# Attention's input product in pairs of column chunks: four of five 1024-column units by a seven-product scheme

## The chip, the cores and the metric

One core of a Trainium2 chip runs one program, a two-layer encoder of 256 tokens and width 2048. TensorE (PE) multiplies into PSUM, VectorE (DVE) and ScalarE (ACT) do the elementwise work, GpSimd (POOL) some of it, and DMA queues bring every weight from HBM. The metric is the device time of the whole program in microseconds, the median of three runs.

## The reference, cut to what matters

The change touches the first product of layer 0: the normalised input times `w_in` of 5264 columns, which are queries Q (2048), keys K (512), values V (512), the indexer's queries (2048), its key (128) and 16 indexer weights.

```python
hn = rmsnorm(h, norm_mix_g[i])
...
proj = hn @ w_in                       # 256 x 2048 times 2048 x 5264, float32
q = proj[..., :o0].reshape(B, S, N_HEADS, HEAD_DIM)
k = proj[..., o0:o1].reshape(B, S, N_KV, HEAD_DIM)
v = proj[..., o1:o2].reshape(B, S, N_KV, HEAD_DIM)
qi = proj[..., o2:o3].reshape(B, S, IDX_HEADS, IDX_DIM)
ki = proj[..., o3:o4]
wi = proj[..., o4:].astype(jnp.float32) * (IDX_HEADS ** -0.5 * IDX_DIM ** -0.5)
q = rope(q, positions, HEAD_DIM); k = rope(k, positions, HEAD_DIM)
ki = layernorm(ki, kidx_g, kidx_b)
qi = rope(qi, positions, IDX_ROPE); ki = rope(ki, positions, IDX_ROPE)
# indexer scores -> the 64 best keys of each token -> softmax attention over those -> @ w_out
```

After it come a squared-ReLU MLP, a gated embedding, then layer 1 with a convolution in place of attention, and the final norm.

## The kernel before, in words

Activations stand in SBUF transposed, as blocks of 128 features by 256 tokens (two token halves t = 0, 1). A float32 product is made of three fp32r matmuls: activation and weight are each split in a high part (`xh`, `wh`) and a low part (`xl`, `wl`), and high x high, high x low and low x high are added in PSUM. The high part of a weight tile is made by ACT (L322), the low part by DVE (L323), both in `halves`. A weight tile `raw` is 128 x 2 x 512 floats (512 KB); there are nine raw buffers (`RAWS`) and six pairs of split buffers (`SPLITS`).

`gemm` (L369) makes one chunk of up to 512 columns: 16 feature blocks x 2 token halves x 3 = 96 matmuls and 8 weight tiles. `pair_gemm` (L215), which before serves the MLP and the gate products only, makes two chunks at once. Of the 16 feature blocks 8 go through a seven-product scheme (Strassen's form by Winograd): pairs of blocks, token halves and chunks form 2 x 2 block matrices, and seven products on sums of activations and sums of weights replace eight. That is 7 x 4 x 3 = 84 matmuls for 96; the other 8 blocks take 96 as always, so a pair takes 180 for 192. The weights' sums are made in the raw tiles, by a DMA that adds while it writes (issued by POOL, L261) or by DVE (L263); each sum is split again, so a pair has 22 splits for 16. The activations' sums (L191 to L203, class `Sums`) are made once per activation.

In attention, before, all ten chunks go through `gemm`: V, K, a chunk of 400 columns (256 indexer queries, the indexer's key, the 16 weights), the indexer's queries in 512 + 512 + 512 + 256, then Q in four of 512. The input `x` comes in four chunks of 512 features; each is transposed on PE (L428), scaled and split by ACT (L382) and DVE (L383), while the first product already runs. The constant vectors of later layers are loaded by `vectors` (L146 to L157): five small DMAs on ACT's queue (L150), then one transpose on PE (L155) and a copy on DVE (L156).

Every engine works its own queue in order. The order of the work is set by `defer` and `step` (a piece of work runs so many steps later) and then by the framework's scheduler, which lays out each engine's list when the program is built. What stands on an engine behind a waiting instruction waits too; ACT's DMA issues are in ACT's list.

## Time and profile before

| | |
|---|---|
| median of three runs | 2248.43 us (2247.61 to 2248.62) |
| the profiled execution | 2248.04 us |
| its span, first to last instruction | 2246.3 us |
| PE busy | 2224.4 us, 99% of the span |
| DVE busy | 1874.4 us, 83% |
| ACT busy | 1432.1 us, 64% |
| mean granted TensorE clock | 0.998 |

A profile row gives an engine, a line of the kernel, the operation, what it writes `<-` reads, and shapes. The matmuls overlap, so the duration of one is no price; the distance from start to start is. The same holds in a small way on ACT and DVE, where the next instruction starts some 0.1 us before the last one's recorded end. Idle time stands in brackets with what ended it.

### The profile page before, as it was taken

What the parts mean: (1) busy time and instruction counts of PE and PEld (TensorE: products, weight loads), DVE (VectorE), ACT (ScalarE), POOL (GpSimd) and SP (SyncE); (2) the same over time, 40 slices, a digit from 0 to 9 for tenths busy, and PEclk for the clock granted to TensorE, in tenths of its full rate; (3) what the DMA queues carried; (4) which work ended last, traced back from release to release, by engine and by line L of the source; (5) the groups of instructions that cost most, each with busy time, mean ns of one, the idle gap of its engine ahead of it and who ended that gap; (6) DMA issues with size and microseconds to landing.
All of it is one profiled execution on the core that took longest, in us unless ns stands there. A gap on an engine that the chain in (4) does not pass through costs nothing.

```text
span 2246.3 us, 29595 instructions
## 1 busy us (share of the span) xinstructions
PE 2224.4 (99%) x10366; PEld 1847.5 (82%) x10366; DVE 1874.4 (83%) x2516; ACT 1432.1 (64%) x1920; POOL 428.6 (19%) x313
## 2 busy tenths in 40 slices
PE   9999999999999999999999999999999999999998
PEld 7888778888888888888898887888888888888886
DVE  5658657988888888889868999789889889889987
ACT  6545546765765765766765744577567577577675
POOL 0201210111011011011139872111111101101012
PEclk9999999999999999999999999999999999999999
DMA  8655446887887887887767552677877877877884
GB/s 278 198 150 171 148 128 169 224 249 204 234 242 203 238 240 202 243 232 202 205 194 226 181 175 67 201 199 201 275 205 202 271 201 209 270 196 216 237 245 121
DMA packets 268021, 463.42 MB, mean 206 GB/s; under 512 B 16340, under 2 KB 62308, under 8 KB 267744
## 3 DMA queue, kind: packets, MB, share of 16 engines
q1 hardware_dynamic: 225840, 381.88, 50.9%
q0 software_dynamic: 39168, 75.51, 20.1%
q10 hardware_dynamic: 2864, 4.15, 0.6%
q8 instruction: 81, 1.33, 0.2%
q14 instruction: 68, 0.56, 0.1%
HBM read 459.38 MB, written 2.10 MB: 205 GB/s over the span
## 4 chain that ended last, share of the span: by engine, by line
PE 93%; DVE 4%; issue 1%; DMA 1%; ACT 1%; POOL 0%; SPq 0%; POOLq 0%; DVEq 0%; ACTq 0%
PE pm L238 42%; PE at L238 21%; PE pm L347 8%; PE pm L349 8%; PE pm L348 8%; PE pt L763 1%; DVE at L950 1%; PE at L808 1%; DVE wl L323 1%; PE pt L428 1%; PE at L612 0%; PE at L659 0%; PE at L689 0%; DMA work<-in_b_w_dw 0%; DMA raw<-in_a_w_in 0%
## 5 line engine op out<-in xcount | busy, mean ns | idle before, releaser
L322 ACT ACTIVATE wh<-raw 128x1024 fp32r<-128x1024 f32 (+2 forms) x1032 | 1058.8, 1040 | 621.8 <-PE at L238 187.8
L323 DVE TENSOR_TENSOR wl<-raw,wh 128x1024 fp32r<-128x1024 f32 (+1 forms) x955 | 1146.5, 1223 | 267.1 <-ACT wh L322 250.6
L261 POOL DMA_DIRECT2D raw<-in_mlp_w x128 | 155.1, 1212 | 1203.1 <-DVE wl L323 1076.3
L238 PE MATMUL pm<-wl,xhA 128*128 128x512 f32 x504 | 197.7, 392 | 0.0
L238 PE MATMUL pm<-wl,xhB 128*128 128x512 f32 x504 | 197.5, 392 | 0.0
L238 PE MATMUL pm<-wh,xlB 128*128 128x512 f32 x504 | 196.4, 391 | 0.0
L238 PE MATMUL pm<-wh,xlA 128*128 128x512 f32 x504 | 196.4, 391 | 0.0
L238 PE MATMUL pm<-wh,xhB 128*128 128x512 f32 x504 | 192.5, 392 | 0.0
L238 PE MATMUL pm<-wh,xhA 128*128 128x512 f32 x504 | 192.3, 393 | 0.0
L347 PE MATMUL pm<-wh,xhA 128*128 128x512 f32 (+2 forms) x480 | 184.1, 388 | 1.4 <-ACT xhA L382 0.6
L349 PE MATMUL pm<-wh,xlA 128*128 128x512 f32 (+2 forms) x480 | 183.6, 387 | 0.5 <-DVE xlA L1041 0.5
L348 PE MATMUL pm<-wl,xhA 128*128 128x512 f32 (+2 forms) x480 | 183.8, 384 | 0.0
L263 DVE TENSOR_TENSOR raw<-raw 128x1024 f32<-128x1024 f32 x144 | 175.5, 1220 | 1.0
L323 POOL TENSOR_TENSOR wl<-raw,wh 128x1024 fp32r<-128x1024 f32 (+1 forms) x77 | 158.3, 2079 | 30.2 <-ACT wh L322 29.1
L347 PE MATMUL pm<-wh,xhB 128*128 128x512 f32 (+1 forms) x448 | 163.1, 365 | 0.0
L348 PE MATMUL pm<-wl,xhB 128*128 128x512 f32 (+1 forms) x448 | 162.0, 362 | 0.0
L349 PE MATMUL pm<-wh,xlB 128*128 128x512 f32 (+1 forms) x448 | 161.8, 363 | 0.0
L950 DVE SCALAR_TENSOR_TENSOR at<-u,wdw,at 128x256 f32<-128x256 f32 x402 | 160.5, 483 | 0.0
L238 PE MATMUL at<-wh,xlA 128*128 128x512 f32 x360 | 140.9, 391 | 0.0
L238 PE MATMUL at<-wh,xhA 128*128 128x512 f32 x360 | 140.8, 391 | 0.0
L238 PE MATMUL at<-wh,xlB 128*128 128x512 f32 x360 | 140.8, 391 | 0.0
L238 PE MATMUL at<-wh,xhB 128*128 128x512 f32 x360 | 140.7, 391 | 0.0
(228 smaller groups left out, 3951.1 us busy)
## 6 DMA issues: line engine op xcount, KB each, us to landing
raw<-in_mlp_w SPq DMA_DIRECT2D x448, 512.0 KB, 5.4
raw<-in_mlp_w POOLq DMA_DIRECT2D x128, 512.0 KB, 6.4
raw<-in_a_w_in SPq DMA_DIRECT2D x72, 512.0 KB, 4.1
raw<-in_ple_w_gate SPq DMA_DIRECT2D x56, 512.0 KB, 5.6
raw<-in_b_w_pw SPq DMA_DIRECT2D x96, 256.0 KB, 3.1
raw<-in_a_w_out SPq DMA_DIRECT2D x32, 512.0 KB, 3.7
raw<-in_b_w_pw SPq DMA_DIRECT2D x32, 512.0 KB, 4.3
raw<-in_ple_w_gate POOLq DMA_DIRECT2D x16, 512.0 KB, 6.2
```

The costliest lines, as they stand in the source:

```text
L238: nc.tensor.matmul(bank[v], l, r, start=v not in begun, stop=bool(left[v] == 0 or (last and j == 2)), skip_group_check=v in again)
L261: nc.gpsimd.dma_start(r, piece(*rows(other, q)), accum_op=ALU.add)
L263: nc.vector.tensor_tensor(r, r, raw(other, q), op=ALU.add)
L322: recent[0] = nc.scalar.activation(wh, r, AF.Copy).ins
L323: (low or nc.vector).tensor_tensor(wl, r, wh.bitcast(F32), op=ALU.subtract)
L347: nc.tensor.matmul(pm[t][:, :n], a, wh[:, i], start=k + i == 0, stop=False)
L348: nc.tensor.matmul(pm[t][:, :n], a, wl[:, i], start=False, stop=False)
L349: nc.tensor.matmul(pm[t][:, :n], b, wh[:, i], start=False, stop=k + i == kt - 1)
L428: nc.tensor.transpose(pt[:, k, t, :], h[:, t, (kk + k) * P:(kk + k + 1) * P], ident)
L763: nc.tensor.transpose(pt[:, k, t, :], both[t][:, 2 * j + k, :], ident)
L808: nc.tensor.matmul(pp, l, r[:, k], start=k == 0 and j == 0, stop=k == 1 and j == 2)
L950: nc.vector.scalar_tensor_tensor(dst, src, w, z, op0=ALU.mult, op1=ALU.add)
```

## The change: what it does

The ten chunks become five units. K and V, the first and the second half of the indexer's queries, and the first half of Q each are a pair of chunks through `pair_gemm`; the second half of Q stays two `gemm` chunks, and the chunk of 400 columns shrinks to 144 (the indexer's key and the weights), since the 256 columns of indexer queries go into a pair. A new class `Beside` holds the activation's blocks as before, and five of the seven sums beside them, in the tiles that attention's output takes later. The paired feature blocks are the last eight instead of the first eight. The first pair begins with two plain groups (`begin=2`), and `x` is loaded in the order 0, 2, 3, 1. `rotated` and `two_chunks` take a finished bank through a copy on ACT and a sum on DVE to the old rotation; `LATE` puts the second head group's attention four steps later. One of the two `at` banks is held by a pair, and part of the indexer's dot products (`dots`) go to the transpose banks. The squares for the norm are put off by some steps.

In the whole program PE has 10182 matmuls for 10230: in attention 48 more of 512 columns, 96 of 144 in place of 96 of 400, and 96 of 256 gone. DVE and ACT have 32 more splits of a full weight tile each (and 8 of 144 columns for 8 of 400 and 8 of 256), DVE 16 more sums of weight tiles, 16 more sums of banks and some 28 more small instructions; POOL issues 16 more adding DMAs.

Two places of the order matter below. The first is ACT's list around the five vector loads (L150 before, L153 now). Before, they stand between the scaled copies and splits of the first weight tiles (`xhA` is the high part of a transposed `x` block, `wh` of a weight tile, `work ... ssq` a square for the norm):

```order
L322 ACTIVATE wh_273<-raw_271 128x1024
L401 ACTIVATE work_307,ssq_111<-h_79 128x512
L401 ACTIVATE work_309,ssq_111<-h_79 128x512
L150 DMA work_77<-in_norm_mlp_g 32x128
L382 ACTIVATE xhA_109<-pt_226,vcol_87 128x256
L382 ACTIVATE xhA_109<-pt_235,vcol_87 128x256
L150 DMA work_77<-in_b_ln_g 16x128
L322 ACTIVATE wh_313<-raw_311 128x1024
L150 DMA work_77<-in_b_ln_b 16x128
L150 DMA work_77<-in_b_b_dw 16x128
L150 DMA work_77<-in_b_b_pw1 32x128
L322 ACTIVATE wh_331<-raw_329 128x1024
```

Now ACT's list has them behind its twelfth split, behind eight squares and behind two copies of banks (L615), the last of which reads the bank `pm_152` that PE fills with the third of the seven products of the first pair:

```order
L450 ACTIVATE work_368,ssq_111<-h_79 128x512
L450 ACTIVATE work_388,ssq_111<-h_79 128x512
L615 ACTIVATE held_332<-at_149 128x512
L450 ACTIVATE work_390,ssq_111<-h_79 128x512
L615 ACTIVATE held_428<-pm_152 128x512
L153 DMA work_77<-in_norm_mlp_g 32x128
L153 DMA work_77<-in_b_ln_g 16x128
L153 DMA work_77<-in_b_ln_b 16x128
L153 DMA work_77<-in_b_b_dw 16x128
L153 DMA work_77<-in_b_b_pw1 32x128
L371 ACTIVATE wh_480<-raw_296 128x1024
```

So the five loads have moved from the first five weight tiles of the program to the middle of the first pair, behind an instruction that waits for PE.

The second is PE's list around the transpose that those loads feed (L155 before, L158 now). Before:

```order
L348 MATMUL pm_382<-wl_441,xhA_109 128x512
L349 MATMUL pm_382<-wh_440,xlA_110 128x512
L347 MATMUL pm_383<-wh_440,xhA_109 128x512
L348 MATMUL pm_383<-wl_441,xhA_109 128x512
L349 MATMUL pm_383<-wh_440,xlA_110 128x512
L155 MATMUL at_456<-ident_80,work_77 128x112
L347 MATMUL pm_382<-wh_461,xhA_109 128x512
L348 MATMUL pm_382<-wl_462,xhA_109 128x512
L349 MATMUL pm_382<-wh_461,xlA_110 128x512
L347 MATMUL pm_383<-wh_461,xhA_109 128x512
```

`pm_382` and `pm_383` are banks of the second chunk, whose matmuls go on behind the transpose. Now:

```order
L281 MATMUL at_149<-wh_298,xlB_114 128x512
L281 MATMUL pm_152<-wl_413,xhB_113 128x512
L281 MATMUL pm_152<-wh_412,xlB_114 128x512
L281 MATMUL pm_152<-wh_412,xhB_113 128x512
L281 MATMUL pm_152<-wl_413,xhB_113 128x512
L281 MATMUL pm_152<-wh_412,xlB_114 128x512
L158 MATMUL at_492<-ident_80,work_77 128x112
L281 MATMUL at_149<-wh_452,xhB_113 128x512
L281 MATMUL at_149<-wl_453,xhB_113 128x512
L281 MATMUL at_149<-wh_452,xlB_114 128x512
L281 MATMUL at_149<-wh_452,xhB_113 128x512
L281 MATMUL at_149<-wl_453,xhB_113 128x512
```

`at_492` is the transpose's bank; `pm_152` is the bank of the copy above and `at_149` the pair's fourth bank, which goes on with a twice summed weight tile (`raw_283` in the split `wh_452`). The transpose has moved from behind 132 matmuls of 512 columns to directly behind the last matmul into `pm_152`: before it now stand 18 warming transposes, 33 transposes of inputs and 72 matmuls of 512 columns, and between the last matmul that the copy waits for and the transpose stands nothing.

The diff, cut to its core:

```diff
@@ -79,8 +81,9 @@
         return ps_tr.tile([P, NB], F32, name="pt", tag="tr")
 
     def at_tile(which=None):
+
         if which is None:
-            turns[0] ^= 1
+            turns[0] = 1 - (turns[0] if unit_bank[0] is None else unit_bank[0])
             which = turns[0]
         return ps_at.tile([P, NB], F32, name="at", tag=f"at{which}")
 
...
+    def five(kk, pt, g):
+
+        y, z, v = work(4, P), work(4, P), work(2, P)
+        for k, dst in ((0, v), (1, z[:, 1:3, :])):
...
+        tt(y[:, 1, :], x11, y[:, 3, :], op=ALU.subtract)
+        tt(z[:, 0, :], x12, y[:, 1, :], op=ALU.subtract)
+        return y, z
+
+    class Beside:
+
+
+
+        def __init__(self, x, other):
+            self.x = x
+            self.five = []
+            for p in "hl":
+                v = acts.tile([P, KT, S], F32R, name="x" + p + other, tag="x" + p + other).rearrange("p k s -> p (k s)")
+                self.five.append(v[:, :5 * SP * P].rearrange("p (m i f) -> p m i f", m=5, i=SP))
+            self.paired, self.plain = KT - 2 * SP, range(KT - 2 * SP)
+
+        def block(self, part, k, t):
+            return self.x[part][:, k, t * P:(t + 1) * P]
+
+        def sums(self, part, m, i):
+            return self.five[part][:, m, i, :] if m < 5 else self.block(part, self.paired + 2 * i + 1, m - 5)
+
+        def put(self, kk, pt, g):
+            put_blocks([v[:, kk:kk + 2, :] for v in self.x], pt, g[:, kk:kk + 2])
+            if kk >= self.paired:
+                y, z = five(kk, pt, g)
+                i = (kk - self.paired) // 2
+                for m, n, src in ((0, 4, y), (4, 1, z[:, :1, :])):
+                    split(self.five[0][:, m:m + n, i, :], self.five[1][:, m:m + n, i, :], src)
...
-    def pair_gemm(x, src, taken, extras=(), apart=False):
+    def pair_gemm(x, src, take, extras=(), apart=False, begin=0):
...
-        bank = {"x": at_tile(), "y": mm_tile(), "v": mm_tile(), "z": mm_tile()}
+        mine = 1 - (turns[0] if unit_bank[0] is None else unit_bank[0])
+        unit_bank[0] = mine
+
+        def taken(what, b):
+            take(what, b)
+            if what == "x" and unit_bank[0] == mine:
+                unit_bank[0] = None
+
+        bank = {"x": at_tile(mine), "y": mm_tile(), "v": mm_tile(), "z": mm_tile()}
         begun, again, left = set(), set(), {"x": 3 * SP, "y": SP, "v": SP, "z": 2 * SP}
         for v in left:
-            left[v] += KT - 2 * SP
+            left[v] += len(x.plain)
             left[v] *= 3
...
         def rows(name, q):
-            return range(2 * q.start + (name in "cd"), 2 * q.stop, 2), int(name in "bd")
+            return range(x.paired + 2 * q.start + (name in "cd"), x.paired + 2 * q.stop, 2), int(name in "bd")
...
-        ks = groups(2 * SP, KT - 2 * SP)
+        ks = groups(x.plain.start, len(x.plain))
+        n1 = [lambda r=r: plain(0, r) for r in ks]
+
+        def more(n):
+            for _ in range(n):
+                n1.pop(0)()
+
+        more(begin)
         seven(0, "x", "a", part="x1")
         add("a", "b")
         seven(5, "y", "c")
-        for r in ks[:-2]:
-            plain(0, r)
+        more(len(n1) - 2 if not begin else 1)
         seven(3, "z", "a", part="z1")
         add("a", "d")
         seven(4, "z", "d")
         add("d", "b")
         seven(1, "x", "a", part="x2")
         add("a", "c")
-        plain(0, ks[-2])
+        more(len(n1) - 1)
         seven(6, "v", "a")
         seven(2, "x", "d", part="x3")
-        plain(0, ks[-1])
+        more(len(n1))
         for r in ks:
             plain(1, r)
         return rest
...
@@ -461,19 +510,22 @@
...
+    xS = Beside(xA, "B")
+
     def first(c):
-        h_half(4 * c, xA, gcol["mix0"])
-        h_half(4 * c + 2, xA, gcol["mix0"])
-        defer(SQ_LAG, lambda: norm.add(c, recent[0]))
+        h_half(4 * c, xS, gcol["mix0"])
+        h_half(4 * c + 2, xS, gcol["mix0"])
 
     load_x(0)
     pv = at_tile()
     nc.tensor.transpose(pv[:, :32], vrow[0][:32, :], ident[:32, :32])
     nc.vector.tensor_copy(vcol[:, :32], pv[:, :32])
     first(0)
-    for c in range(1, 4):
-        defer(2 * c - 1, lambda c=c: load_x(c))
-        defer(2 * c, lambda c=c: first(c))
+    for c, load, turn in ((2, 1, 2), (3, 2, 2), (1, 3, 4)):
+        defer(load, lambda c=c: load_x(c))
+        defer(turn, lambda c=c: first(c))
+    for c in range(4):
+        defer(4 + c, lambda c=c: norm.add(c, recent[0]))
     defer(8, vectors)
...
+        def two_chunks(n0, ends, begin=0):
+
+            rs = {}
+
+            def taken(what, bank):
+                if what in EARLY:
+                    rs[EARLY[what]] = held(4, P)
+                    nc.scalar.activation(rs[EARLY[what]].rearrange("p h d -> p (h d)"), bank, AF.Copy)
+                    return
+                (t, n), r = WHERE[what], rs[what]
+                rf = r.rearrange("p h d -> p (h d)")
+                nc.vector.tensor_tensor(rf, bank, rf, op=ALU.subtract if what in MINUS else ALU.add)
+                ends[n](t, r)
+            pair_gemm(xS, blocks(w_in, n0, 2 * NB), taken, begin=begin)
...
+        def rotated(rot, make, then):
+
+            toks = {}
+
+            def end(t, r):
+                nc.scalar.activation(r, r, AF.Copy, scale=norm0[t])
+                rope(r, t, 4, rot)
+                toks[t] = r
+                if len(toks) == TT:
+                    dst = make()
+                    turn_heads(toks, dst)
+                    then(dst)
+            return end
...
         norm0 = norm
         vv = att.tile([P, TT, NB], F32, name="vv")
-        pm = gemm(xA, blocks(w_in, V0))
-
-        def values(pm=pm):
-            for t in range(TT):
...
         kT = att.tile([P, 4, S], F32, name="kT")
-        pm = gemm(xA, blocks(w_in, K0))
-        defer(0, lambda pm=pm: heads(pm, 128, kT))
+        defer(12, angles)
+
+        def values(t, r):
+            nc.scalar.activation(vv[:, t, :], r.rearrange("p h d -> p (h d)"), AF.Copy, scale=norm0[t])
+        two_chunks(K0, (rotated(128, lambda: kT, lambda dst: None), values), begin=2)
...
-        pm = gemm(xA, blocks(w_in, KI0 - 256, 400))
+        pm = gemm(xA, blocks(w_in, KI0, 144))
...
         defer(0, index_keys)
-        defer(0, lambda pm=pm: heads(pm, 64, qT_last[:, 2:4]))
...
         def dots(j, qT, t):
             per = NB // KS[t]
             for q in range(0, 4, per):
-                pa = at_tile()
+                pa = at_tile() if q == 0 else tr_tile()
...
-        for j in range(4):
-            pm = gemm(xA, blocks(w_in, QI0 + j * NB, NB if j < 3 else 256))
-
-            def index_heads(j=j, pm=pm):
-                qT = att.tile([P, 4, S], F32, name="qT", bufs=2) if j < 3 else qT_last
-                heads(pm, 64, qT if j < 3 else qT[:, :2])
-                defer(3, lambda: dots(j, qT, 0))
-                defer(4, lambda: dots(j, qT, 1))
-            defer(0, index_heads)
...
+        def index_heads(j):
+            def then(qT):
+                defer(3, lambda: dots(j, qT, 0))
+                defer(4, lambda: dots(j, qT, 1))
+                if j == 3:
+                    defer(5, lambda: select(0))
+                    defer(6, lambda: select(1))
+            return rotated(64, head_tile, then)
+
+        def head_tile():
+            return att.tile([P, 4, S], F32, name="qT", bufs=2)
+
+        for j in range(0, 4, 2):
+            two_chunks(QI0 + j * NB, (index_heads(j), index_heads(j + 1)))
...
+        def attention(g, qT, late=0):
             def go(t):
                 lgs = logits(g, qT, t)
                 defer(2, lambda: attend(g, lgs, t))
-            defer(2, lambda: go(0))
-            defer(3, lambda: go(1))
+            defer(2 + late, lambda: go(0))
+            defer(3 + late, lambda: go(1))
+
+        def query_heads(g, pm):
+            qT = head_tile()
+            heads(pm, 128, qT)
+            attention(g, qT)
...
-        for g in range(N_KV):
+        two_chunks(Q0, [rotated(128, head_tile, lambda qT, g=g: attention(g, qT, LATE * g)) for g in range(2)])
+        xB = xpair("B")
+        for g in range(2, N_KV):
             pm = gemm(xA, blocks(w_in, Q0 + g * NB))
             defer(0, lambda g=g, pm=pm: query_heads(g, pm))
```

## Rows read from the trace of the kernel before

**Rows 1.** the page: share of the chain that ended last, by engine

```profile
PE 93%; DVE 4%; issue 1%; DMA 1%; ACT 1%; POOL 0%; SPq 0%; POOLq 0%; DVEq 0%; ACTq 0%
```

**Rows 2.** windows: stretch, length, busy us (count) per engine, clock, DMA share, GB/s

```profile
8.00:25.00 17.00, 14.99 (x58) 11.42 (x58) 10.66 (x16) 12.02 (x26) 0.00 (x0) 1.00 1.00 362
40.00:330.00 290.00, 290.00 (x1416) 242.42 (x1415) 187.81 (x303) 150.88 (x244) 50.69 (x58) 1.00 0.54 165
500.00:540.00 40.00, 40.00 (x178) 33.11 (x177) 34.62 (x34) 22.47 (x23) 4.85 (x5) 1.00 0.86 252
```

**Rows 3.** timeline of PE, 512, 400, 256 columns, transposes, float32: start, length

```profile
111.68 0.39 PE L347 MATMUL pm<-wh,xhA 128*128 128x512 f32 x1
...
114.18 0.39 PE L349 MATMUL pm<-wh,xlA 128*128 128x512 f32 x1
...
62.10 0.34 PE L348 MATMUL pm<-wl,xhA 128*128 128x400 f32 x1
...
66.07 0.34 PE L349 MATMUL pm<-wh,xlA 128*128 128x400 f32 x1
...
153.54 0.28 PE L348 MATMUL pm<-wl,xhA 128*128 128x256 f32 x1
...
156.18 0.28 PE L349 MATMUL pm<-wh,xlA 128*128 128x256 f32 x1
...
20.60 1.04 PE L428 MATMUL pt<-ident,h 128*128 128x128 f32 x8
...
120.51 1.02 PE L612 MATMUL at<-kiT,qT 128*128 128x256 f32 x4
```

**Rows 4.** timeline of ACT in the first 35 us: rows that give distances

```profile
1.76 0.45 ACTq L490 DMA_DIRECT2D kg<-in_a_kidx_g  x1
...
7.66 0.46 ACT L382 ACTIVATE xhA<-pt,vcol 128x256 fp32r<-128x256 f32 x1
...
12.17 0.82 ACT L382 ACTIVATE xhA<-pt,vcol 128x256 fp32r<-128x256 f32 x2
...
31.53 2.94 ACT L322 ACTIVATE wh<-raw 128x1024 fp32r<-128x1024 f32 x3
```

**Rows 5.** groups of ACT over the span: count, busy, mean ns

```profile
L744 ACT ACTIVATE held<-at 128x512 f32<-128x512 f32 x48 | 28.4, 592 | 19.8 <-PE at L238 19.8
...
L401 ACT ACTIVATE work<-h 128x512 f32<-128x512 f32 x40 | 24.9, 622 | 10.8 <-DVE h L826 7.0 <-DMA h<-in_x 3.7
```

**Rows 6.** DMA issues: queue, count, KB, us to landing

```profile
pos_i<-in_positions ACTq DMA_DIRECT2D x1, 1.0 KB, 2.3
work<-in_norm_mix_g SPq DMA_DIRECT2D x1, 16.0 KB, 1.7
work<-in_norm_mlp_g ACTq DMA_DIRECT2D x1, 16.0 KB, 6.2
```

**Rows 7.** timeline of PE: its 73rd matmul of 512 columns, and a gap

```profile
33.58 0.73 PE L347 MATMUL pm<-wh,xhA 128*128 128x512 f32 x2
34.88 0.50 PE L347 MATMUL pm<-wh,xhA 128*128 128x512 f32 x1 [0.57 <-ACT xhA L382]
```

**Rows 8.** windows around the fall of the granted clock, columns as in rows 2

```profile
1370.00:1372.70 2.70, 1.48 (x8) 0.67 (x6) 2.09 (x8) 0.00 (x0) 0.00 (x0) 1.00 0.00 0
1372.70:1376.20 3.50, 2.93 (x13) 2.66 (x14) 2.18 (x5) 1.10 (x3) 0.69 (x1) 0.51 0.00 0
```

**Rows 9.** timeline of DVE in the first 40 us

```profile
8.15 0.48 DVE L383 SCALAR_TENSOR_TENSOR xlA<-pt,vcol,xhA 128x256 fp32r<-128x256 f32 x1 [2.21 <-ACT xhA L382]
8.96 0.88 DVE L383 SCALAR_TENSOR_TENSOR xlA<-pt,vcol,xhA 128x256 fp32r<-128x256 f32 x2 [0.32 <-ACT xhA L382]
...
37.41 2.36 DVE L323 TENSOR_TENSOR wl<-raw,wh 128x1024 fp32r<-128x1024 f32 x2
```

**Rows 10.** groups of DVE over the span: sums of activations, and their low parts

```profile
L197 DVE TENSOR_TENSOR work<-work 128x128 f32<-128x128 f32 x48 | 13.7, 286 | 0.0
...
L380 DVE TENSOR_TENSOR xlB<-work,xhB 128x512 fp32r<-128x512 f32 x24 | 16.0, 684 | 0.0
```

More of the change, by code (lines that the diff above doesn't have):

```diff
@@ L54 @@
 HELD = 8
+LATE = 4
 WHERE = {"y": (0, 0), "z": (0, 1), "v": (1, 0), "x": (1, 1)}
@@ L73, in encoder @@
     turns = [0]
+    unit_bank = [None]
     def mm_tile():
@@ L177, in __init__ @@
             self.rest = [v[:, n:].rearrange("p (k s) -> p k s", s=S) for v in self.main]
+            self.paired, self.plain = 0, range(2 * SP, KT)
         def block(self, part, k, t):
@@ L190, in put @@
                 return
-            y, z, v = work(4, P), work(4, P), work(2, P)
-            for k, dst in ((0, v), (1, z[:, 1:3, :])):
-                nc.scalar.activation(dst, pt[:, k], AF.Copy, scale=g[:, kk + k:kk + k + 1] if g is not None else 1.0)
-            x11, x21, x12, x22 = v[:, 0, :], v[:, 1, :], z[:, 1, :], z[:, 2, :]
-            tt = nc.vector.tensor_tensor
-            nc.vector.tensor_scalar(y[:, 0, :], x11, -1.0, None, op0=ALU.mult)
-            tt(y[:, 2, :], x21, x11, op=ALU.subtract)
-            tt(y[:, 3, :], x21, x22, op=ALU.subtract)
-            tt(y[:, 1, :], x11, y[:, 3, :], op=ALU.subtract)
-            tt(z[:, 0, :], x12, y[:, 1, :], op=ALU.subtract)
+            y, z = five(kk, pt, g)
             i = kk // 2
@@ L203, in put @@
                 split(dst[0][:, :, i, :], dst[1][:, :, i, :], src)
+    def five(kk, pt, g):
+        y, z, v = work(4, P), work(4, P), work(2, P)
+        for k, dst in ((0, v), (1, z[:, 1:3, :])):
+            nc.scalar.activation(dst, pt[:, k], AF.Copy, scale=g[:, kk + k:kk + k + 1] if g is not None else 1.0)
+        x11, x21, x12, x22 = v[:, 0, :], v[:, 1, :], z[:, 1, :], z[:, 2, :]
+        tt = nc.vector.tensor_tensor
+        nc.vector.tensor_scalar(y[:, 0, :], x11, -1.0, None, op0=ALU.mult)
+        tt(y[:, 2, :], x21, x11, op=ALU.subtract)
+        tt(y[:, 3, :], x21, x22, op=ALU.subtract)
+        tt(y[:, 1, :], x11, y[:, 3, :], op=ALU.subtract)
[16 more added lines that the diff above has]
+            if kk >= self.paired:
+                y, z = five(kk, pt, g)
+                i = (kk - self.paired) // 2
+                for m, n, src in ((0, 4, y), (4, 1, z[:, :1, :])):
+                    split(self.five[0][:, m:m + n, i, :], self.five[1][:, m:m + n, i, :], src)
     def put_blocks(x, pt, g):
@@ L418, in put @@
     def put(x, kk, pt, g=None):
-        if isinstance(x, Sums):
+        if isinstance(x, (Sums, Beside)):
             x.put(kk, pt, g)
@@ L542, in heads, with turn_heads @@
                 rope(toks[t], t, nh, rot)
+            turn_heads(toks, dst)
+        def turn_heads(toks, dst):
             def turn():
-                for i in range(nh // 2):
+                for i in range(dst.shape[1] // 2):
                     pt = tr_tile().rearrange("p (k t f) -> p k t f", k=2, t=TT)
@@ L551, in heads @@
             defer(1, turn)
+        def two_chunks(n0, ends, begin=0):
[18 more added lines that the diff above has]
+                    dst = make()
+                    turn_heads(toks, dst)
+                    then(dst)
+            return end
         norm0 = norm
         vv = att.tile([P, TT, NB], F32, name="vv")
[L556 to L562 removed]
         kT = att.tile([P, 4, S], F32, name="kT")
[L566 to L567 removed]
+        defer(12, angles)
+        def values(t, r):
+            nc.scalar.activation(vv[:, t, :], r.rearrange("p h d -> p (h d)"), AF.Copy, scale=norm0[t])
+        two_chunks(K0, (rotated(128, lambda: kT, lambda dst: None), values), begin=2)
         kiT = att.tile([P, S], F32, name="kiT")
         wi = att.tile([P, TT, 16], F32, name="wi")
[L572 to L573 removed]
+        pm = gemm(xA, blocks(w_in, KI0, 144))
         def index_keys(pm=pm):
@@ L577, in index_keys @@
             for t in range(TT):
-                nc.vector.tensor_scalar(wi[:, t, :], pm[t][:, 384:400], norm0[t], WI_SCALE,
+                nc.vector.tensor_scalar(wi[:, t, :], pm[t][:, 128:144], norm0[t], WI_SCALE,
                                         op0=ALU.mult, op1=ALU.mult)
                 ki = att.tile([P, 1, P], F32, name="ki", bufs=2)
-                nc.scalar.activation(ki[:, 0, :], pm[t][:, 256:384], AF.Copy, scale=norm0[t])
+                nc.scalar.activation(ki[:, 0, :], pm[t][:, :128], AF.Copy, scale=norm0[t])
                 st = small.tile([P, 6], F32, name="st")
@@ L692, in attend @@
             split(xB[0][sl], xB[1][sl], po.rearrange("p (h q) -> p h q", h=4))
-        def query_heads(g, pm):
-            qT = att.tile([P, 4, S], F32, name="qT", bufs=2)
-            heads(pm, 128, qT)
+        def attention(g, qT, late=0):
             def go(t):
@@ L803, in project @@
                         w.append(halves(r))
[L804 removed]
+                    (wh, wl), pp = w[0], at_tile()
                     for k in range(2):
```

8 lines of the change are left out of this document (removed).

## The prediction

> **What bounds the kernel now.** First the chain that ended last: 93% of it is PE [rows 1], so the time is PE's work plus the places where PE waits. Then the windows, for where those are. From 40 to 330 us, nearly all of the stage that the change touches, PE is busy 290.00 of 290.00 us while DVE is at 187.81 and ACT at 150.88 [rows 2]. In the first 40 us it is otherwise: from 8 to 25 us the DMA engines are at a share of 1.00, PE is short of full, and DVE and ACT, with 10.66 and 12.02 of 17 us, wait for data in turn [rows 2]. So a matmul saved after 40 us is worth its whole distance, a wait put on PE costs its whole length, and what DVE and ACT get more of is free after 40 us as long as they keep ahead, but not in the start.
>
> **PE's work.** The price of a matmul is the distance of starts [rows 3]. At 512 columns 11 distances take 2.50 us, 227 ns (a record of 0.39 us thus runs 0.16 past the next start). At 400 columns the two rows are 22 matmuls apart: 3.97 us, 180 ns. At 256 columns 22 again: 2.64 us, 120 ns. There is no fp32r matmul of 144 columns. The straight line through the three gives 73 ns; the 256-column row, 120 ns, is a bound from above if the price falls with the width. Every PE instruction here loads 128 columns of weights, and the narrowest of these, the transposes of 128 columns, start (1.04 - 0.16) / 8 = 110 ns apart, with the same overrun at the end of the eight. I take 110, the row nearest in width. The sum: 48 x 227 = 10.9 us more, 96 x 180 = 17.3 and 96 x 120 = 11.5 less, 96 x 110 = 10.6 more: 7.3 us less. With 73 ns it is 10.9 less.
>
> The Trainium skill, "TensorE: Matmul & The Clock Gate", section "Back-to-back issue gap", gives a matmul alone N / 2.4 + 2.5 ns: 62.5 ns for 144 columns, and the sum of this forecast would be 4.6 us lower by it. For 512 columns it gives 215.8 ns where the rows have 227, so the trace is above the rule, and the narrow matmuls are where the same page's load of 128 weight columns could show; I keep the rows.
>
> **The start: ACT's list.** PE's list now has the transpose of the constant vectors (L158) right behind the 72nd matmul of 512 columns, and it waits for five small loads that stand in ACT's list behind two copies of banks. Nothing on PE can pass it. Until the loads ACT has, by the order: 24 scaled blocks of 256 columns (16 to the high part, 8 for the sums) at 0.82 - 0.46 = 0.36, 8.6 (the first of two neighbours gives 0.10 to the second); 12 splits of a weight tile at (2.94 - 0.10) / 3 = 0.95, 11.4 [both rows 4]; 4 high parts of 512 at 0.53 and 4 of 128 at an estimated 0.2 (the 592 ns of a 512-column copy [rows 5] less the 0.1 that neighbours overlap, and a share of it), 2.9; 8 squares at 0.62 [rows 5], 5.0; 2 copies of a bank at 0.5 [rows 5], 1.0. Together 28.9 us. ACT's first scaled block started at 7.66 [rows 4], so 36.6 without a wait. It will wait: in 8 to 25 us before it idled 17 - 12.02 = 5.0 us [rows 2], and now it works for data at the same rate; I take 6, with 1 and 9 as ends. Then 42.6. Five issues at up to 0.45 [rows 4]: 44.8. A small load lands 1.7 to 6.2 us after its issue [rows 6], the long one in the saturated stretch; by 44 us the weight tiles wait for free buffers, so I take 2.3. **The transpose starts at 47.1 us**, with ends of 41 and 54.
>
> Before, PE's 73rd matmul started at 33.58, and after it PE lost another 0.57 to a late `xhA` [rows 7], which is hidden now. The start therefore costs 47.1 - 33.6 - 0.6 = **12.9 us**.
>
> DVE is not far behind. Up to the 15th split, which 103 matmuls stand ahead of, its list has 16 low parts of 256 columns at 0.88 - 0.48 = 0.40 and 15 splits at (2.36 - 0.08) / 2 = 1.14 [both rows 9], four sums of weight tiles at the same 1.14, 20 small sums at 0.20 or less and 8 low parts of the five sums at 0.60 and 0.20 (the durations less the same 0.08 [rows 10]), and 1.8 of angles: 36.8 us. From 8.15 [rows 9], with 5 us of idle (6.3 before in 8 to 25 us [rows 2]), that is 49.9. Before, that many matmuls were done at 33.58 + 31 x 0.227 + 0.57 = 41.2. So if the loads cost nothing, DVE's list still puts PE 8.7 us late. If they come at 47, DVE waits behind its copy of the transpose too, but has by then split what the next 12 matmuls need, and the rest, 5.8 us, runs under PE's 7 us.
>
> **The clock.** PE's last matmul before the transpose follows DVE's ninth split, 24.2 us of its list, so near 8.15 + 24.0 + 5 = 37.2, plus six matmuls 38.6. It then stands idle to 47.1. In the stretch from 1370 to 1372.7, where PE was busy 1.48 of 2.7 us, the granted clock fell to 0.51 (1.2 GHz of 2.4) and stayed there for 3.5 us [rows 8]. I expect the same once: half of 3.5, **1.7 us**; ends 0 and twice that.
>
> **The rest of attention.** DVE gets, beyond the first pair and over all, 36 us of splits, 18 of weight sums and 10 of bank sums, less 10 for the narrower splits, so its 187.81 of 290 becomes some 242 of 283, 85%. The MLP's pairs run with DVE at 34.62 of 40 and PE at 40.00 [rows 2], so it is covered on the mean; the top-64 selection now falls into a pair that wants its splits faster. The adding DMAs, the copies of banks and the single free `at` bank are the MLP's own pattern, which runs full. I allow **0.7 us**, between 0 and 4. Less than 0: no, PE has no gap there to win.
>
> **The sum.** 2248.04 (the profiled execution, its span and 1.7 us around it) - 7.3 + 12.9 + 1.7 + 0.7 = 2256.0; the median of the runs is 0.4 higher, so **2256**. This kernel's measurement can tell about 0.2%, 4.5 us, from no change; the forecast is 0.35% slower.
>
> **Rivals.** B, no slower: the small loads are covered. If ACT idles 1 us and a load lands in 1.7, the transpose comes at 41 us; then DVE's list decides, PE is 8.7 us late in gaps too short for the clock, and the time is 2248.4 - 7.3 + 8.7 + 0.7 = 2250.5. It decides where the transpose starts before 42.5. For it: the loads are tiny, and the DMA engines are free of queue by then. Against it: 28.9 us of ACT's own work, which needs no guess of idle time.
> C, slower still: the narrow matmuls do not run at fp32r's pace. The float32 matmuls take (1.02 - 0.16) / 4 = 0.215 us for 256 columns [rows 3], with two instructions to each product; 144 columns would be 0.24 us, 12.5 us more, 2269. For it: no row below 256 columns. Against it: 400 and 256 lie on one line with 512.
> D, faster: the start costs nothing and PE's 7.3 us count in full, 2241. It needs the transpose before about 37 us, where ACT's own work alone ends at 36.6; only if much of that work came late in the list could it be. That the change does not save what it says is no rival: the count of matmuls is the program's own.
>
> **How the numbers follow.** Forecast 0.65, B 0.21, C 0.07, D 0.07. Forecast and C are slower by over 0.2%: 0.72; B is within: 0.21; D faster: 0.07. The range is 2246 to 2265: below it lies D, above it C and the case of a load that lands after 6 us with ACT idling 9; between them are B, the line's 73 ns (3.6 us less) and the 4 us for the rest. The forecast's own range is 2251 to 2263.
>
> **What would show it.** A gap on PE ahead of L158, ended by a DMA of a vector, of 5 to 10 us, with 512-column matmuls about twice as far apart for some us after it; ACT's copy of `pm_152` near 42 us; PE's 73rd matmul of 512 columns near 47. The 144-column matmuls 110 ns apart. From 60 to 320 us PE full, and attention's end some 8 us later than before. I am wrong in mechanism if PE passes L158 without a gap, wrong in size if the gap is there but the loads land at once, and wrong in the whole if PE shows gaps of its own in the later pairs.

## The result, and the profile after

The changed kernel takes 2264.45 us, median of 4 runs (2264.24 to 2265.55), the kernel before on the same chip 2248.02; the ratio is 1.0074, 95% interval 1.0057 to 1.0092. It is slower, as forecast, but by 16.4 us where 8 had been forecast (2256); it lies near the upper edge of the range (2246 to 2265) and outside the forecast's own (2251 to 2263). The profiled execution has a span of 2262.5 us for 2246.3.

To say where the 16.2 us of span come from, each distance between the starts of two neighbouring matmuls is compared with the undisturbed distance of its form (fp32r of 512, 400, 256 and 144 columns 227, 180, 120 and 112 ns, a transpose 109, float32 of 256 columns 215); what is over counts as lost in its stretch. The span is PE's work plus what is lost (one profiled execution of each kernel; every number is rounded by itself):

| us lost | before | after | more |
|---|---|---|---|
| 0 to 60 us | 11.4 | 26.0 | 14.6 |
| 60 to 240 | 1.0 | 0.9 | -0.1 |
| 240 to 340 | 0.9 | 8.5 | 7.6 |
| 340 to 420 | 1.9 | 1.7 | -0.2 |
| from 420 | 13.0 | 14.5 | 1.4 |
| all | 28.3 | 51.6 | 23.3 |

PE's work is therefore 16.2 - 23.3 = 7.1 us less. The page's share of the chain still names PE alone, which is true and says nothing of where it waits [rows 1]:

```profile
PE 93%; DVE 3%; ACT 1%; DMA 1%; issue 1%; POOL 0%; SPq 0%; ACTq 0%; POOLq 0%; DVEq 0%
```

The windows of [rows 2] again (stretch, length, busy us per engine, clock, DMA share), then the stretch of the selection:

```profile
8.00:25.00 17.00, 12.36 (x43) 8.78 (x44) 11.13 (x22) 10.54 (x19) 2.55 (x2) 0.72 1.01 358
40.00:330.00 290.00, 280.82 (x1339) 231.21 (x1339) 233.70 (x356) 181.51 (x283) 66.74 (x67) 0.98 0.64 182
500.00:540.00 40.00, 40.00 (x178) 33.12 (x177) 35.32 (x36) 23.05 (x22) 4.81 (x4) 1.00 0.83 235
```

```profile
205.00:246.00 41.00, 41.00 (x194) 34.13 (x193) 40.79 (x88) 24.42 (x36) 10.48 (x9) 1.00 0.65 201
```

The clock of 0.72 against 1.00 in the first row makes the two starts look more different than they are: before, too, matmuls of 512 columns start 0.43 us apart until 17.6 us, which is half speed by their distance.

PE, full from 40 to 330 before, misses 9.2 us there. DVE's mean over the stretch is 81%, near the 85% forecast; but in the 41 us in which selection, splits and the bank sums of the paired queries meet, it is full to 0.2 us while PE still has no gap. That this is what makes the softmaxes late is not shown: before, DVE was nearly as full around its selection (the window below), and PE waited for nothing behind it.

```profile
187.00:214.00 27.00, 27.00 (x129) 22.51 (x128) 26.34 (x69) 12.60 (x15) 4.31 (x4) 1.00 0.55 164
```

The narrow matmuls (timeline of PE, starts 22 matmuls apart) stand (78.22 - 75.76) / 22 = 112 ns apart, for the 110 taken [rows 3]:

```profile
75.76 0.27 PE L397 MATMUL pm<-wl,xhA 128*128 128x144 f32 x1
...
78.22 0.27 PE L398 MATMUL pm<-wh,xlA 128*128 128x144 f32 x1
```

The start, on PE and on ACT ([rows 4] and [rows 7] are its rows before):

```profile
39.81 0.40 PE L281 MATMUL pm<-wh,xlB 128*128 128x512 f32 x1
46.59 0.42 PE L158 MATMUL at<-ident,work 112*128 112x112 f32 x1 [6.38 <-DMA work<-in_b_b_pw]
46.69 0.78 PE L281 MATMUL at<-wh,xhB 128*128 128x512 f32 x1
```

```profile
40.35 0.63 ACT L450 ACTIVATE work<-h 128x512 f32<-128x512 f32 x1
40.50 0.34 ACTq L153 DMA_DIRECT2D work<-in_norm_mlp_g  x1
...
42.28 0.87 ACTq L153 DMA_DIRECT2D work<-in_b_b_pw  x1
...
43.49 0.59 ACT L615 ACTIVATE held<-at 128x512 f32<-128x512 f32 x1
...
44.58 0.59 ACT L615 ACTIVATE held<-pm 128x512 f32<-128x512 f32 x1
```

The loads are issued between ACT's squares (L450) from 40.5 on, the last lands 4.2 us after its issue, and PE stands 6.4 us. So the loads were not held by the copies of banks, behind which ACT's list has them: all five are issued before the first copy runs, at 43.49, and the copy of `pm_152` follows only at 44.58. The kernel before shows the same: its first load leaves at 21.75, while the two squares listed ahead of it run at 23.00 and 23.61.

```profile
21.75 0.34 ACTq L150 DMA_DIRECT2D work<-in_norm_mlp_g  x1
...
23.00 0.62 ACT L401 ACTIVATE work<-h 128x512 f32<-128x512 f32 x1
...
23.61 0.62 ACT L401 ACTIVATE work<-h 128x512 f32<-128x512 f32 x1
```

In either kernel an issue in ACT's list thus left before the activations listed ahead of it had run. And the loads are not the only thing that PE needs there: the matmul behind L158 writes the bank `at` that the first copy empties, and that copy ends at 44.08, so of the 6.4 us the loads alone account for 2.5.

The end of attention, on PE: logits (L735), the transposes of the softmax (L760), and what the gaps wait for.

```profile
295.75 1.02 PE L735 MATMUL at<-kT,qT 128*128 128x256 f32 x4
298.80 0.79 PE L396 MATMUL pm<-wh,xhB 128*128 128x512 f32 x1 [2.02 <-ACT held L593]
...
328.17 1.03 PE L735 MATMUL at<-kT,qT 128*128 128x256 f32 x4
...
329.96 0.60 PE L760 MATMUL pt<-ident,held 128*128 128x128 f32 x4
331.93 0.66 PE L760 MATMUL pt<-ident,held 128*128 128x128 f32 x4 [1.37 <-POOL held L749]
...
334.79 0.50 PE L396 MATMUL pm<-wh,xhB 128*128 128x512 f32 x1 [1.34 <-ACT xhB L428]
```

Between the last logits and the first transposes behind them stand 4 matmuls of 512 columns; the softmax needs DVE, ACT and POOL in turn, and PE waits for each. The gap ahead of 298.80 is a bank that ACT has not yet copied (L593), its copy standing behind exponentials in ACT's list. The clock fell again behind such gaps; ahead of its first fall below, PE had waited for ACT's scaled copies (L204), 1.31 us up to 20.78 and 1.02 up to 22.45 (first line: PE's waits from 15 to 60 us; then windows, columns as above; [rows 8] before):

```profile
PE pt L477 <- ACT work L204: 2.3, 2, 1.3
```

```profile
22.30:29.10 6.80, 6.56 (x16) 4.81 (x17) 6.80 (x14) 5.93 (x12) 1.21 (x1) 0.50 1.09 302
42.80:49.60 6.80, 3.00 (x8) 2.46 (x9) 5.21 (x12) 4.27 (x10) 2.47 (x2) 0.50 1.06 224
298.80:302.20 3.40, 3.40 (x8) 2.73 (x9) 2.22 (x6) 2.48 (x9) 1.61 (x3) 0.50 0.59 204
1387.60:1394.40 6.80, 6.30 (x25) 5.50 (x25) 4.91 (x10) 3.73 (x8) 0.69 (x1) 0.50 0.01 2
```

The last of these is layer 1's, which before lasted 3.5 us. Around it, from 1340 to 1420 us, 0.8 us more are lost than before; the rest of the 1.4 lost more from 420 us on lies scattered.

### The profile page after: what moved, and what is told of

The parts are those of the page before. It is cut to its first block, busy times and chain, and to the rows that moved or that the text cites. A ratio compares the mean times of both kernels' runs of the same rounds, so it can differ in the third digit from the quotient of the medians.

```text
span 2262.5 us, 29673 instructions
## 1 busy us (share of the span) xinstructions
PE 2226.6 (98%) x10318; PEld 1842.7 (81%) x10318; DVE 1932.3 (85%) x2596; ACT 1467.5 (65%) x1974; POOL 447.5 (20%) x325
## 4 chain that ended last, share of the span: by engine, by line
PE 93%; DVE 3%; ACT 1%; DMA 1%; issue 1%; POOL 0%; SPq 0%; ACTq 0%; POOLq 0%; DVEq 0%
PE pm L281 47%; PE at L281 24%; PE pm L396 6%; PE pm L398 5%; PE pm L397 5%; PE pt L843 1%; DVE at L1030 1%; PE at L888 1%; PE pt L477 1%; ACT wh L371 1%; DVE wl L372 1%; PE at L765 0%; PE pt L604 0%; DMA raw<-in_a_w_in 0%; PE at L735 0%
## 5 line engine op out<-in xcount | busy, mean ns | idle before, releaser
L371 ACT ACTIVATE wh<-raw 128x1024 fp32r<-128x1024 f32 (+1 forms) x1056 | 1082.6, 1040 | 606.2 <-PE at L281 218.3
L372 DVE TENSOR_TENSOR wl<-raw,wh 128x1024 fp32r<-128x1024 f32 (+1 forms) x979 | 1177.4, 1227 | 230.2 <-ACT wh L371 214.6
L281 PE MATMUL pm<-wl,xhA 128*128 128x512 f32 x632 | 249.8, 396 | 0.0
L281 PE MATMUL pm<-wh,xlA 128*128 128x512 f32 x632 | 248.2, 395 | 0.0
L281 PE MATMUL pm<-wh,xhA 128*128 128x512 f32 x632 | 243.9, 397 | 3.4 <-ACT wh L371 3.4
L306 DVE TENSOR_TENSOR raw<-raw 128x1024 f32<-128x1024 f32 x160 | 195.4, 1223 | 1.1
L281 PE MATMUL at<-wh,xhB 128*128 128x512 f32 x408 | 161.3, 395 | 0.1
L281 PE MATMUL at<-wl,xhB 128*128 128x512 f32 x408 | 160.5, 393 | 0.0
L281 PE MATMUL at<-wl,xhA 128*128 128x512 f32 x392 | 153.3, 391 | 0.0
L281 PEld LDWEIGHTS pm<-wh,xhA 128*128 128x128 f32 x632 | 119.4, 189 | 28.9 <-ACT wh L371 4.3
```

The costliest lines, as they stand in the source:

```text
L281: nc.tensor.matmul(bank[v], l, r, start=v not in begun, stop=bool(left[v] == 0 or (last and j == 2)), skip_group_check=v in again)
L306: nc.vector.tensor_tensor(r, r, raw(other, q), op=ALU.add)
L371: recent[0] = nc.scalar.activation(wh, r, AF.Copy).ins
L372: (low or nc.vector).tensor_tensor(wl, r, wh.bitcast(F32), op=ALU.subtract)
```

## The experiments

All times are medians; the kernel before ran beside each, 2247.3 to 2248.0, and "ratio" is to it. "Lost" is counted as above, in one profiled execution of each; for e12 and e13, whose attention ends later, the column goes to 345 us. The last column counts the falls of the clock from 240 to 345 us; each is 3.4 us long and so accounts for up to 1.7 us of what is lost there.

| kernel | us | ratio, interval | lost 0 to 60 | lost 240 to 340 | falls |
|---|---|---|---|---|---|
| after | 2264.45 | 1.0074, 1.0057 to 1.0092 | 26.0 | 8.5 | 1 |
| e1_vec_late | 2262.68 | 1.0069, 1.0054 to 1.0084 | 25.3 | 6.9 | 0 |
| e2_kv_plain | 2256.85 | 1.0048, 1.0031 to 1.0065 | 10.8 | 10.0 | 1 |
| e3_index_first | 2262.51 | 1.0068, 1.0053 to 1.0083 | 25.5 | 6.5 | 0 |
| e4_q_plain | 2259.27 | 1.0053, 1.0038 to 1.0068 | 25.4 | 1.8 | 0 |
| e5_late0 | 2261.93 | 1.0060, 1.0046 to 1.0073 | 25.4 | 6.6 | 0 |
| e6_held10 | 2261.15 | 1.0057, 1.0043 to 1.0070 | 23.2 | 8.5 | 1 |
| e7_squares_late | 2261.86 | 1.0060, 1.0046 to 1.0074 | 21.1 | 11.5 | 2 |
| e9_two_pairs | 2247.09 | 0.9994, 0.9985 to 1.0003 | 11.2 | 1.7 | 0 |
| e10_q_plain_late | 2261.53 | 1.0062, 1.0047 to 1.0077 | 25.2 | 3.0 | 0 |
| e11_two_pairs_begin | 2245.47 | 0.9990, 0.9981 to 0.9999 | 10.6 | 1.7 | 0 |
| e12_adds_by_dma | 2269.28 | 1.0093, 1.0079 to 1.0107 | 28.6 | 11.6 | 2 |
| e13_q2_low_pool | 2270.03 | 1.0099, 1.0082 to 1.0116 | 26.8 | 12.8 | 2 |

**The start.** First the wait that the trace names.

```diff
-    defer(8, vectors)
+    defer(40, vectors)
```

> The five small vector loads and the transpose L158 go 32 steps later; nothing else. My theory (PE stands 6.6 us at L158 for loads that wait in ACT's list; behind it DVE's list has 3 to 4 us less delay): the gap ahead of L158 goes, the lost time of the first 60 us falls from 26.0 to about 20, the time is 2258 (2257 to 2260). Rival (data and splits are late anyway, the stall only moves into other gaps): the lost time falls by under 2 us, 2262.5 or more. If all of the start's cost hung on L158 it would be 2250.

My theory missed. The gap at L158 is gone, and a gap of 3.9 us stands at 45.05 in its place; the start loses 0.6 us less. (The other 1.6 of this run are the clock, which did not fall at 298 us; the gaps there are the same.) PE and ACT of e1:

```profile
45.05 0.79 PE L281 MATMUL at<-wh,xhB 128*128 128x512 f32 x1 [3.94 <-ACT held L615]
```

```profile
43.18 0.63 ACT L450 ACTIVATE work<-h 128x512 f32<-128x512 f32 x1
...
43.79 0.63 ACT L450 ACTIVATE work<-h 128x512 f32<-128x512 f32 x1
...
44.40 0.59 ACT L615 ACTIVATE held<-at 128x512 f32<-128x512 f32 x1
```

The copy that frees PE's bank stands behind the squares in the same list. So those went too:

```diff
-        defer(4 + c, lambda c=c: norm.add(c, recent[0]))
+        defer(11 + c, lambda c=c: norm.add(c, recent[0]))
```

> As e1_vec_late, and the eight squares of the norm (5 us of ACT) 7 steps later as well, out of the way of ACT's two copies of banks. Theory L (in e1 the 4.1 us gap at 45 us was ACT's list again, with DVE busy 21.8 of 22 us just behind): the gap shrinks but DVE's splits take its place, the loss of the first 60 us falls from 25.3 to 22 to 24, 2260 to 2262. Rival (ACT's list alone is the start's cost): the loss falls by 4 us or more, to 21 or less, 2258.

The start lost 4.2 us less than e1, as the rival said (its 2258 was not reached); up to 1.7 of that is the clock, whose second fall lasts 3.4 us (42.3 to 45.7) for 6.9 in e1. PE still waits for the same copy (2.1 us, at 41.9), and DVE is full (window of e7):

```profile
25.00:47.00 22.00, 19.34 (x68) 13.94 (x67) 21.89 (x42) 18.57 (x40) 2.43 (x2) 0.84 0.64 135
```

PE's own waits in e7 (5 to 60 us), though, name ACT for 7.4 us and DVE for 0.5:

```profile
PE pm L281 <- ACT wh L371: 3.0, 1, 3.0
PE pt L477 <- ACT work L204: 2.3, 2, 1.3
PE at L281 <- ACT held L615: 2.1, 1, 2.1
PE pm L281 <- DVE wl L372: 0.5, 1, 0.5
```

The time hardly moved, since a gap of 3.9 us opened at the end of attention with the other order. Next the first pair itself:

```diff
-        two_chunks(K0, (rotated(128, lambda: kT, lambda dst: None), values), begin=2)
+        pm = gemm(xA, blocks(w_in, V0))
+        defer(0, values)
+        pm = gemm(xA, blocks(w_in, K0))
+        defer(0, lambda pm=pm: heads(pm, 128, kT))
+    # the five sums from a second transpose of x, at steps 20, 22, 24, 26
```

> K and V are two plain units again, as before, with the order of the start as before, and the five sums are made from step 20 on, from transposes done a second time (16 more of 128 columns, 1.8 us). My theory (the start's 14.6 us come from the work that a paired first unit puts ahead of its matmuls): 14.6 less, 2.7 more for 12 matmuls and 1.8 more for the transposes, 2254 (2252 to 2257); the loss from 280 to 340 us stays. Rival (the sums cost the same wherever they are made, by crowding ACT and DVE): 2261 or more.

The start is back at 10.8. The time is 2.9 us above my number, for 3.9 us lost near 89 us, where the next pair waits for sums made too late, and 1.5 more at the end. The start's 14.6 us belong to the paired first unit together with what was arranged for it: e2 also puts back the order of `x`, the squares and the angles, and takes the five sums out of the start, so it does not part these. To see whether DVE's list is what is left in e7, four of its sums of weight tiles went to the DMA queues:

```diff
-                if other == "b":
+                if other == "b" or begin:
```

> As e7_squares_late, and in the first pair the four sums of weight tiles that DVE makes (1.14 us each) are made by adding transfers, as the other four are. Theory D (what is left of the start's loss in e7, 21.1 against 11.4 before, is DVE's list, busy 21.9 of 22 us from 25 to 47): the loss of the first 60 us falls by 3 to 4.6 us, to 16.5 to 18. Rival (data or ACT are as late): it falls by under 1.5, to 19.6 or more, or grows with the bytes that are fetched twice. The time depends on the end of attention too, 2256 to 2260.

It lost 7.4 us more, up to 3.4 of them by one more fall of the clock (54.0 to 60.9 us). DMA's share from 25 to 47 us rose from 0.64 to 0.99, and from 47 to 60 DVE was idle for want of data (windows of e12):

```profile
25.00:47.00 22.00, 17.97 (x65) 12.91 (x66) 20.48 (x47) 19.30 (x41) 6.12 (x6) 0.89 0.99 221
47.00:60.00 13.00, 9.05 (x27) 6.44 (x27) 5.59 (x10) 8.27 (x14) 1.95 (x2) 0.76 0.70 134
```

So here the bytes are the next limit. What binds the last 9.7 us of e7 is not shown by this run: DVE's 21.89 of 22 speaks for its list, PE's waits speak for ACT's, and it stays open.

**The end of attention.** First the selection, which ends at 246 us for 214 before.

```diff
-        two_chunks(K0, ...)          # K and V
-        ...                          # index keys, 144 columns
-        for j in range(0, 4, 2): two_chunks(QI0 + j * NB, ...)
+        two_chunks(QI0, ..., begin=2)
+        ...                          # index keys, then the dots of heads 0 and 1
+        two_chunks(QI0 + 2 * NB, ...)
+        two_chunks(K0, ...)
```

> Order of the units: index queries 0 and 1, index keys, index queries 2 and 3, K and V, then the queries; so the top-64 selection has a unit more ahead of the first logits. Theory S (the 7.7 us lost from 280 to 340 us come from the selection, which ends at 246 us against 214 before and shifts the softmaxes to the end): the loss there falls to under 2 us, the time to 2258 (2256 to 2260). Rival T (two head groups that end together, and the LATE turns, crowd the end whatever the selection does): the loss stays over 5 us, 2262 or more.

The loss fell by 2.0 only, and up to 1.7 of that is the clock, which did not fall near 298 us here; theory S does not carry it, and the bounds of rival T hold. But the test was weaker than meant: the scheduler spread the selection from 171 to 237 us, so the first logits came at 233 us, for 230 in the changed kernel. Then the pair of queries, undone:

```diff
-        two_chunks(Q0, [rotated(128, head_tile, ...LATE * g) for g in range(2)])
         xB = xpair("B")
-        for g in range(2, N_KV):
+        for g in range(N_KV):
```

> The queries of groups 0 and 1 are two plain units again; the other three pairs stay. PE has 12 matmuls more, 2.7 us. If the pair of queries is what slows the selection and crowds the end (S and T alike): the loss from 280 to 340 us falls by 5 us or more, 2262 (2260 to 2263). Rival I (the index pairs alone, whose dots end 17 us later, are enough): the loss stays, 2267.

The loss is 1.8, so 6.7 less, up to 1.7 of it the clock, which does not fall there; and with 2.7 us more of PE's work the time is 2259.27, even below the 2262 expected. The end of e4 on PE has 18 matmuls between the last logits and the first transposes, 4.3 us from 320.62 to 324.95, and one small gap:

```profile
319.95 1.02 PE L735 MATMUL at<-kT,qT 128*128 128x256 f32 x4
320.62 0.58 PE L396 MATMUL pm<-wh,xhB 128*128 128x512 f32 x1
...
324.95 0.60 PE L760 MATMUL pt<-ident,held 128*128 128x128 f32 x4
...
330.55 0.50 PE L396 MATMUL pm<-wh,xhB 128*128 128x512 f32 x1 [0.49 <-ACT xhB L428]
```

What is it in the pair? `LATE = 0` for 4 starts group 1 sooner:

> LATE is 0: the logits of group 1 come 4 steps earlier. Theory C (two query groups whose tokens are ready together, a unit later than plain ones, leave too few plain matmuls behind the first logits to cover four softmaxes): starting group 1 earlier helps a little, the loss from 280 to 340 us falls from 8.1 to 3 to 6 us, 2260 to 2262. Theory H (the eight held buffers, taken by the pair's four tokens and the logits of two groups, hold the copy of group 2's product, 24 us behind its last matmul): the buffers fill sooner, the loss stays at 8 or grows, 2264 or more.

2261.93, lost 6.6, a little past C's band. But PE's waits from 240 us on are 4.4 us for 4.8 in the changed kernel; the rest of the difference is the clock, which did not fall near 298 us, so `LATE` hardly matters. `HELD = 10`, `RAWS = 8`, for 8 and 9:

> Ten held buffers in place of eight, paid for with one raw weight buffer less (8 for 9), which by the full PE of the later stages should cost nothing or a few tenths in the start. Theory H: the copy of group 2's product follows its last matmul by under 8 us in place of 24, the loss from 280 to 340 us falls from 8.1 to under 3, 2258 to 2260. Theory C: the loss stays over 6, 2263 or more.

Theory H falls: 8.5, and the copy of group 2's product still comes at 270 us. (With one raw buffer less the start even lost 2.8 us less; its two later falls of the clock last 3.4 us each, for 6.8.) Then e4 with the softmaxes put off as the pair does it:

```diff
-            attention(g, qT)
+            attention(g, qT, (9, 4, 0, 0)[g])
```

> As e4_q_plain (all query groups plain), but the logits of group 0 are put off by 9 steps, a unit's length, and those of group 1 by 4, which is about when they come with the pair. Theory C (it is the time at which the softmaxes start, with fewer plain matmuls left to cover them, not the pair's work): the loss from 240 to 340 us, 1.8 in e4, comes back to 5 us or more, 2262 to 2266. Rival (the pair's own splits and sums on DVE and ACT): it stays under 3, 2259 to 2261.

3.0 for 1.8, neither with a fall of the clock: lateness alone gives 1.2 of the 5.0 or more that undoing the pair takes away beside the clock, and theory C as I put it falls. Last, less work for DVE where it is full:

```diff
-            pm = gemm(xA, blocks(w_in, Q0 + g * NB))
+            pm = gemm(xA, blocks(w_in, Q0 + g * NB), low=(lambda k: nc.gpsimd) if g == 2 else None)
```

> The changed kernel with one edit: the eight low parts of the weights of query group 2 are made by GpSimd, so DVE, busy 40.8 of 41 us from 205 to 246, has some 9 us less to do there. Theory D (DVE is full while selection, splits and sums of the paired queries are due together, so the softmaxes start late and bunch up at the end): the loss from 240 to 340 us falls from 8.5 to 5 or less, 2259 to 2261. Rival (the order written for the pair loses the time whatever DVE does): 7.5 or more, 2263 to 2265; if GpSimd is too slow for the splits, PE waits for it between 222 and 250 and the time is above 2265.

GpSimd was too slow, 2602 ns for a low part (the group below) where DVE takes 1231 in the same run, and PE lost 7 us more between 220 and 260. So DVE got little of the room that the test needed, busy 39.4 of the 41 us for 40.8. The Trainium skill ("GPSIMD Engine Reference", section "Engine selection") says about twice as slow for two inputs; here 2.1 times, so the trace agrees.

```profile
L372 POOL TENSOR_TENSOR wl<-raw,wh 128x1024 fp32r<-128x1024 f32 x8 | 20.6, 2602 | 21.9 <-ACT wh L371 21.9
```

More telling are PE's waits from 240 us on, first of the changed kernel, then of e13 (waited for, us, times, longest):

```profile
PE pm L396 <- ACT held L593: 2.0, 1, 2.0
PE pt L760 <- POOL held L749: 1.5, 2, 1.4
PE pm L396 <- ACT xhB L428: 1.3, 1, 1.3
```

```profile
PE at L735 <- DVE held L738: 3.0, 1, 3.0
PE pm L396 <- ACT held L593: 2.0, 1, 2.0
PE pt L760 <- POOL held L749: 1.4, 1, 1.4
PE pm L396 <- ACT xhB L428: 1.3, 1, 1.3
```

The last three are the same to 0.1 us, though in e13 the selection ended 5 us sooner and all came 7 us later; e1 and e6 have them too. Where a run changes more they differ in size (at the transposes of the softmax the longest is 3.9 us in e2 and e7). But all nine kernels with the pair of queries have a wait of 1.3 us or more there for POOL's `held`, and the four without it, e4, e9, e10 and e11, have none. Waits that come back whatever happens before them seem made where they stand: by what each engine's list puts between a result and its use. That is argued, not shown, since no run changes the list alone; why the pair has this effect, and so a rule for foreseeing it, is open.

**A version that gains.** Pairs where neither the start nor the softmaxes are: V with the first index queries, and the next two.

```diff
+        pm = gemm(xA, blocks(w_in, K0))                    # plain, first
+        pm = gemm(xA, blocks(w_in, KI0 - 256, 400))        # as before
+        two_chunks(V0, (values, index_heads(0)))
+        two_chunks(QI0 + NB, (index_heads(1), index_heads(2)))
+        pm = gemm(xA, blocks(w_in, QI0 + 3 * NB, 256))     # then Q plain, four times
```

> Only two pairs, in the middle of the stage: V with index queries 0, index queries 1 with 2. K is the plain first unit, the index keys stay in a unit of 400 columns, index queries 3 in one of 256, all query groups are plain; the five sums are made from step 10 on from transposes done a second time (the selection is written over the scores to make room for a half of the last index heads). By my account PE has 24 matmuls of 512 columns less (5.4 us) and 16 transposes more (1.8 us), and the losses of the start and of the end are those of before: 2243.7 (2242 to 2246), some 3.6 us below before. Rival (a pair costs its gain wherever it stands, through DVE): 2247 to 2250.

2247.09, not told apart from before. PE's work is 3.9 us less, as counted (span 1.7 less, 2.2 more lost); 2.4 us went at 75 us, where the first pair waits for a sum (1.8) and for a bank to be copied (0.6). The same with `begin=2` for that pair and the sums a step sooner:

> As e9_two_pairs, and the first pair begins with two plain steps, the sums a step earlier: e9 still lost 2.4 us at 75 us to sums that were late. If only that held it: 2.4 less, 2244.7 (2243.5 to 2246), 0.14% below before. Rival (the wait comes back further on, DVE having no room): 2246.5 to 2248.

2245.47, ratio 0.9990 (0.9981 to 0.9999): the wait for the sum is gone, the one for the copy is 0.7, another of 0.6 came at 83.6 us, and the loss over all is 29.9 for 30.5 in e9. It beats the kernel before by 2.0 us or 0.1%, at the edge of what 11 runs can tell, and the changed kernel by some 19.

## Why the prediction was right and wrong, by its steps

**PE's work**: 7.3 us less forecast, 7.1 found; right. The 144-column matmul is 112 ns; rival C's 0.24 us does not hold. The formula of the Trainium skill ("TensorE: Matmul & The Clock Gate", section "Back-to-back issue gap") gives an estimate of 62.5 ns, far below the trace; the section itself says that the formula is for an isolated matmul and under-counts at small N.

**The start**: forecast L158 at 47.1, found 46.59; forecast 12.9 and 1.7 for the clock, 14.6 in all, found 14.6. That the size agrees so well is luck, for errors cancel. ACT's list ran later than forecast: its copy of `pm_152`, expected near 42, started at 44.58. But the loads did not wait for it: the last was issued at 42.28, where the forecast has the issues end at 44.8. And it took 4.2 us to land, for 2.3. Nor does the start hang on L158: without the loads it loses 0.6 less (e1), where the prediction's own account of DVE's list makes 12.9 - 8.7 = 4.2 less. The forecast ended ACT's list at the loads because they were the last thing PE's next instruction needed, and did not ask what the one behind it needs, a bank whose copy ended at 44.08. With the squares late as well 4.2 less are lost (e7), and 9.7 are left. That is near the 8.7 that rival B had for DVE's list, but PE's waits there name ACT, so the nearness shows nothing.

**The clock**: one fall of 3.5 us forecast; in the first 60 us there are two of 6.8 beyond the start's own, the first at 22 us, behind two waits for ACT that I had not foreseen. The sum held because the 12.9 was taken from a time, the 73rd matmul's, that includes this fall; of the second PE worked only 3.00 us, so it cost an estimated 1.5 us, half of that, for the 1.7 forecast.

**The rest of attention**: this term was mis-sized, 0.7 us (0 to 4) for a measured 7.5: 7.6 from 240 to 340 less 0.1 before it. The step that failed is "it is covered on the mean". 85% of DVE over 290 us was right to 4 points, and the pairs themselves run full, as forecast; but the term had nothing at all for the order of the softmaxes behind them, where PE waits 4.8 us and the clock falls once, which is up to 1.7. Undoing the pair of queries takes both away (e4). That it comes of the 41 us at 99.5% which the mean hides is not shown: 27 us at 98% before cost nothing, and the three waits of e13 stayed. I had warned that gaps "in the later pairs" would make me wrong in the whole; they came behind the last pair instead.

**Outside attention**: nothing forecast, 1.2 us found, 0.8 of it around one longer fall of the clock.

Of the 8.4 us between forecast and result, 6.8 are thus the rest of attention, 1.2 what lies outside it, 0.2 PE's work; 0.2 are left by rounding.

## What to carry to other kernels

Taking away the wait that the trace names shows only its distance to the next one: 6.4 us of standing at L158 were worth 0.6. The loads left before activations that stood ahead of them in ACT's list had run, so read from the trace when a load leaves, and not from its place. Before a term is called covered, do not stop at the mean: look at the fullest stretch of the covering engine, and at what the lists put between a result and its use. When two kernels are compared by what PE loses, look at the clock first: one fall more or less is up to 1.7 of the 2.0 us between e3 and the changed kernel. And place such a scheme by what it feeds: a pair as the first unit lost 14.6 us, one ahead of the softmaxes some 5 and a fall of the clock, and the two in the middle of e11 kept 2.0 of the 3.6 us by which they shorten PE's work.
